# First loads in another order, and the last block of an encoder layer closed in two halves of 256 columns

## The chip, the cores and the metric

The kernel runs on one core of a Trainium2 chip. The metric is device time in microseconds (us) of one launch. Three runs of the kernel before took 1307.38, 1307.95 and 1308.11 us, so the median is 1307.95 us.

## What is computed

One encoder layer in float32 on 256 positions (two blocks of 128, called t = 0 and t = 1 here) with a width of 2048:

```python
def mixer_block(x, ...):
    h = rms_norm(x, g_norm)
    uv, qkv, gates = split(h @ w_in)
    y_a = gmlp_branch(uv, ...)            # gelu, LayerNorm, spatial gate
    y_b = neighbourhood_attn(q, k, v, rpb)
    g_a, g_b = split(sigmoid(gates))
    return x + (g_a * (y_a @ w_branch[:1024]) + g_b * (y_b @ w_branch[1024:])) @ w_out
def conv_ffn(x, ...):
    up = conv3(rms_norm(x, g) @ w_up)
    return x + (silu(gate) * val) @ w_down
out = rms_norm(conv_ffn(mixer_block(x)), norm_final)
```

The two ends matter here: the first product, which is the v columns of `h @ w_in`, and the last one, `@ w_down` with its residual, followed by the final RMSNorm.

## The kernel before, in words

**Three products for one.** Every float32 operand is split into a high and a low part in TensorE's fast float32 form. ScalarE (ACT) writes the high part, VectorE (DVE) subtracts it to get the low part, and TensorE (PE) does high x high, low x high and high x low (lines 289 to 291, helper `triple`). A weight piece is 128 rows by 1024 columns, 512 KB; SP loads it as `wraw` (line 126; the first piece in two DMAs of 512 columns, line 124), ACT writes `whi` (line 151) and DVE `wlo` (line 152). Pieces are numbered through the whole program. Five `wraw` buffers and four of `whi` and `wlo` each are turned over.

**The order of the work** is written out by hand. `begin(i)` is called ahead of the products of piece i: it issues the loads up to piece i + 5, does the splits up to piece i + 4 (for the first nine pieces up to the number in `SPLIT_TO`), and runs the tasks that `at(i, ...)` has put down for this piece. `preload[i]` names DMAs that go on SP's queue just ahead of the load of piece i. Each engine executes its instructions in the order in which they are written; SP's and ACT's DMA queues too.

**The start.** The first weight columns, v, are taken with the 16 slices of the transposed x in the order `V_ORDER` = 0, 1, 6, 7, 8, 9, 10, 11, 12, 13, 2, 3, ... Slice k is 128 x 256 values in `xr` (128 KB); `x_split(k)` multiplies it by the norm vector `gmix` and splits it (ACT line 495, DVE line 496, tile `h`). `x_chunk(c)` does slices 2c and 2c + 1; `X_TURN` lists the chunks c and the piece at which each is split, and the order of their loads. ACT's queue loads `gmix` (8 KB) and slice 1; SP's loads slice 0, piece 0 in two halves, piece 1, slices 6 and 7 together, piece 2, slices 2 and 3, piece 3, slices 8 and 9, piece 4, slices 10 and 11, piece 5 and so on. While the first data are on the way, `keep_awake` gives PE 17 transposes of the identity (`WAKE`, line 440).

For some pairs of pieces (`V_QUADS`, pieces 10 to 13 of v) a 2 x 2 block is done in seven products in place of eight. That needs sums of x slices (`act_sums`, lines 295 to 298 and 305, then split in lines 314 and 315) and of weights (lines 324 to 327 and 334, 335); `X_SUMS` says at which piece the sums of x are made. A first statistic of x (`x_norm`, lines 449 to 455) follows at piece 17 on DVE, and after it a gelu on ACT (line 548) with a table load.

**The end.** `run_wide` computes the last 1024 output columns of `@ w_down` in four accumulators `C[t][c]` of 128 x 512, one PSUM bank each. The last four weight pieces (`tail`) are kept back, and then done for one accumulator after the other, 12 products each, so that `finish` can take t = 0, c = 0; then t = 0, c = 1; then t = 1, c = 0; and last t = 1, c = 1. For each `finish` adds the residual (DVE, line 1023), takes the sum of squares (ACT, line 1026, accumulated), and multiplies by the final norm's weights into `y` (DVE, line 1063). After c = 1 follows the root: DVE `pt`, DVE `a` (lines 1069, 1070), ACT `q` = sqrt(a) (line 1071), DVE reciprocal and one Newton step (1072 to 1074). Then `write` scales the 2048 columns of this t in five cuts of 256, 512, 256, 512 and 512, on DVE (line 1085) or ACT (line 1083), and issues five DMAs to the output (line 1089). For t = 0 `write` is put off until after the add and the multiplication of t = 1, c = 0.

Of the kernel before, what the change touches and what calls it, by code (L numbers as in the profile page):

```python
# [8 lines left out]
F32 = mybir.dt.float32  # L9
F32R = mybir.dt.float32r  # L10
AF = mybir.ActivationFunctionType
# [52 lines left out]
def trunk_kernel(ctx, tc, x, x_t, vecs, w_in, ln_g, ln_b, w_st, b_s, rpb, w_branch, w_out, w_up, w_down,  # L64
# [105 lines left out]
    def at(i, f):  # L170
        tasks.setdefault(i, []).append(f)
# [168 lines left out]
    def run_wide(g, tail=0):  # L340
# [8 lines left out]
        def plain(i, t, c):  # L349
            h, l = split_t[i]  # L350
            triple(C[t][c], x_of(order[i - n0], t), h[:, c], l[:, c], i == n0, i == n1 - 1)

# [53 lines left out]

    xr = xin.tile([128, KD, T], F32, name="xr")

# [4 lines left out]
    def load_xt(k, n, queue=None):  # L413
        (queue or nc.sync).dma_start(xr[:, k:k + n], x_t[:, k:k + n])

    gmix = const.tile([128, KD], F32)
    gffn = const.tile([128, KD], F32)
    ck = const.tile([128, 4, 2 * NF], F32)
    nc.scalar.dma_start(gmix, vecs[:, 0:KD])
    load_xt(1, 1, nc.scalar)  # L420

    def load_late():
        nc.sync.dma_start(gffn, vecs[:, KD:2 * KD])
        nc.sync.dma_start(ck.rearrange("p a b -> p (a b)"), vecs[:, 2 * KD:])

# [629 lines left out]

    def finish(ps, t, c):
        x2 = rs["x2"]
        add_down(ps[t][c], t, 2 + c)
        square_columns(t, 2 + c)
        if c == 0:  # L1060
            fin["y", t] = hpool.tile([128, 2, 512], F32, name=f"h{t}")
        y = fin["y", t]
        nc.vector.tensor_mul(y[:, c], x2[:, t, 1024 + c * 512:1536 + c * 512], fin["g", 2 + c])
        if c == 0:
            if t:
                fin["out"]()
            return
        a, r, q, e, pt, both = (const.tile([128, 1], F32, name=f"{n}3{t}") for n in "arqepb")
        nc.vector.tensor_scalar(pt, fin["ss"][:, t, 2:3], 1.0 / D, fin["part"][:, t:t + 1], op0=OP.mult, op1=OP.add)
        nc.vector.tensor_scalar(a, fin["ss"][:, t, 3:4], 1.0 / D, pt, op0=OP.mult, op1=OP.add)  # L1070
        nc.scalar.activation(q, a, AF.Sqrt)
        nc.vector.reciprocal(r, q)
        nc.vector.scalar_tensor_tensor(e, r, r, a, op0=OP.mult, op1=OP.mult)
        nc.vector.tensor_scalar(e, e, -0.5, 1.5, op0=OP.mult, op1=OP.add)

        def write():
            on_act = (3,) if t else (1, 3)
            cuts = (0, 256, 768, 1024, 1536, 2048)
            for n in (0, 1, 2, 3, 4):
                v = x2[:, t, cuts[n]:cuts[n + 1]]  # L1080
                u = y[:, n - 3] if n > 2 else v
                if n in on_act:
                    nc.scalar.activation(v, u, AF.Copy, scale=both)
                else:
                    nc.vector.tensor_scalar(v, u, r, e, op0=OP.mult, op1=OP.mult)
                if n == 0:
                    nc.vector.tensor_mul(both, r, e)
            for n in (0, 1, 2, 3, 4):
                (nc.scalar if n == 3 else nc.sync).dma_start(out[0, t * 128:(t + 1) * 128, cuts[n]:cuts[n + 1]],
                                                             x2[:, t, cuts[n]:cuts[n + 1]])  # L1090

        if t:
            write()
        else:
            fin["out"] = write
# [64 lines left out]
    def down_order(g):  # L1160
# [5 lines left out]
    g_dn = [wide(w_d, 0, down_order(g), g * 1024, lambda k: ff["a"][k], DOWN_QUADS[g], down_room,  # L1166
                 (ev_sums(2 * g, down_room), ev_down if g == 0 else finish), stored=stored, split_room=both_rooms) for g in range(2)]
# [10 lines left out]
    for c, i in X_TURN[1:]:  # L1178
        at(i, lambda c=c: x_chunk(c))
# [111 lines left out]

    fin["ss"] = const.tile([128, NT, 4], F32, name="ss_3")
    at(g_dn[0][1] + 6, open_fin)
    def load_fin():
# [47 lines left out]
```

## Time and profile before

| what | value |
|---|---|
| median of three runs | 1307.95 us (1307.38 to 1308.11) |
| the profiled execution's own time | 1307.83 us |
| its span, first to last instruction | 1306.0 us |
| busy, PE / DVE / ACT / POOL | 1293.6 / 1072.5 / 776.8 / 104.7 us |
| mean granted TensorE clock | 0.997 |
| read from HBM, written | 266.48 MB, 7.34 MB |

A profile is one execution. The profiled execution lies within the three runs, and 1.8 us of its time are outside its span. Times in the trace count from the span's start. In its rows the first number is the start and the second the duration; `SPq` and `ACTq` are the instructions that issue DMAs, and a "landing" is the time from the start of that instruction until the data are in place. PE's matmuls overlap: a 128x512 product is listed with 389 ns, but the next begins 0.23 us after it.

### The profile page before, as it was taken

Reading aid. Unit: us, or ns where it says so; the run is one execution under the profiler, and the core shown is the slowest. Engines: PE = TensorE matmul, PEld = TensorE weight load, DVE = VectorE, ACT = ScalarE, POOL = GpSimd, SP = SyncE. Lnnn points to the kernel's source line nnn. Section 1 sums busy time; section 2 is a strip of 40 time slices with the busy share of each in tenths; the row PEclk is TensorE's granted clock in tenths of the full one; section 3 lists DMA queues with packets and bytes.
Section 4 is the critical chain, followed back from the end, with each engine's and each line's share of the span. In section 5 each row is a group of like instructions: output and inputs, shape, how many; then the busy total and the mean of one; then the engine's idle time right before and its main releaser. Section 6 shows DMA issues by size and latency. Waiting matters only on the chain.

```text
span 1306.0 us, 19254 instructions
## 1 busy us (share of the span) xinstructions
PE 1293.6 (99%) x6712; PEld 1103.9 (85%) x6712; DVE 1072.5 (82%) x1616; ACT 776.8 (59%) x1153; POOL 104.7 (8%) x206
## 2 busy tenths in 40 slices
PE   9999999999999999999999999999999999999997
PEld 7888888888888888888888888888888888888885
DVE  7997777667689966986778878787888889999997
ACT  7766476666655644556556556565555656665563
POOL 0005405413000000000000000000000000000000
PEclk9999999999999999999999999999999999999998
DMA  9779657556556657565566566666666658876782
GB/s 351 251 243 258 191 166 214 175 171 195 177 170 204 218 182 248 202 211 163 177 195 209 182 211 198 215 194 212 191 211 199 215 161 286 288 267 227 265 290 105
DMA packets 174225, 277.19 MB, mean 212 GB/s; under 512 B 13488, under 2 KB 121904, under 8 KB 174128
## 3 DMA queue, kind: packets, MB, share of 16 engines
q1 hardware_dynamic: 165520, 252.28, 59.5%
q0 software_dynamic: 8032, 23.03, 5.5%
q8 instruction: 52, 0.85, 0.3%
q10 hardware_dynamic: 576, 0.66, 0.1%
q14 instruction: 45, 0.37, 0.1%
HBM read 266.48 MB, written 7.34 MB: 210 GB/s over the span
## 4 chain that ended last, share of the span: by engine, by line
PE 96%; DVE 1%; ACT 1%; DMA 1%; issue 0%; SPq 0%; ACTq 0%; DVEq 0%
PE bank L203 31%; PE bank L207 16%; PE bank L291 11%; PE bank L289 11%; PE bank L290 11%; PE bank L231 5%; PE bank L233 4%; PE bank L232 4%; DMA wraw<-in_w_in_dram 1%; PE bank L756 1%; PE bank L806 0%; DVE wlo L152 0%; PE bank L622 0%; PE bank L796 0%; PE bank L887 0%
## 5 line engine op out<-in xcount | busy, mean ns | idle before, releaser
L152 DVE TENSOR_TENSOR wlo<-wraw,whi 128x1024 fp32r<-128x1024 f32 (+1 forms) x472 | 546.0, 1170 | 182.5 <-ACT whi L151 100.4
L151 ACT ACTIVATE whi<-wraw 128x1024 fp32r<-128x1024 f32 (+1 forms) x472 | 470.3, 1010 | 218.4 <-PE bank L290 85.1
L203 PE MATMUL bank<-h,whi 128*128 128x512 f32 x1760 | 425.5, 392 | 0.0
L203 PEld LDWEIGHTS bank<-h,whi 128*128 128x128 f32 x1760 | 322.1, 188 | 61.7
L207 PEld LDWEIGHTS bank<-h,wlo 128*128 128x128 f32 x1760 | 225.9, 191 | 8.8
L207 PE MATMUL bank<-h,wlo 128*128 128x256 f32 x1760 | 228.6, 283 | 0.0
L985 ACT ACTIVATE tc<-ta,ck 128x256 f32<-128x256 f32 x86 | 47.1, 594 | 117.1 <-DVE ta L983 117.1
L291 PE MATMUL bank<-wlo,a 128*128 128x512 f32 x224 | 87.3, 390 | 0.0
L290 PE MATMUL bank<-whi,a 128*128 128x512 f32 x224 | 87.2, 389 | 0.0
L289 PE MATMUL bank<-whi,a 128*128 128x512 f32 x224 | 87.1, 389 | 0.0
L289 PE MATMUL bank<-whi,h 128*128 128x512 f32 x210 | 82.4, 393 | 0.6 <-ACT h L495 0.6
L291 PE MATMUL bank<-wlo,h 128*128 128x512 f32 x210 | 81.9, 390 | 0.7 <-DVE wlo L152 0.7
L290 PE MATMUL bank<-whi,h 128*128 128x512 f32 x210 | 81.8, 390 | 0.8 <-DVE h L496 0.8
L334 ACT ACTIVATE h<-h 128x1024 fp32r<-128x1024 f32 x40 | 40.2, 1053 | 33.7 <-DVE h L326 33.7
L988 DVE SCALAR_TENSOR_TENSOR tc<-ta,ck,tc 128x255 f32<-128x255 f32 x86 | 41.4, 481 | 14.4 <-ACT tc L985 14.4
L231 PE MATMUL bank<-whi,y 128*128 128x512 f32 x128 | 50.5, 394 | 0.0
L231 PE MATMUL bank<-whi,h 128*128 128x512 f32 x128 | 50.4, 394 | 0.0
L233 PE MATMUL bank<-wlo,h 128*128 128x512 f32 x128 | 49.9, 390 | 0.0
L233 PE MATMUL bank<-wlo,y 128*128 128x512 f32 x128 | 49.9, 390 | 0.0
L232 PE MATMUL bank<-whi,y 128*128 128x512 f32 x128 | 49.8, 389 | 0.0
L232 PE MATMUL bank<-whi,h 128*128 128x512 f32 x128 | 49.8, 389 | 0.0
L291 PEld LDWEIGHTS bank<-wlo,a 128*128 128x128 f32 x224 | 42.0, 188 | 9.1 <-DVE wlo L152 0.3
(284 smaller groups left out, 1786.0 us busy)
## 6 DMA issues: line engine op xcount, KB each, us to landing
wraw<-in_w_up_dram SPq DMA_DIRECT2D x336, 256.0 KB, 3.2
wraw<-in_w_in_dram SPq DMA_DIRECT2D x111, 512.0 KB, 4.5
wraw<-in_w_down_dram SPq DMA_DIRECT2D x86, 512.0 KB, 5.4
wraw<-in_w_in_dram SPq DMA_DIRECT2D x66, 256.0 KB, 3.3
wraw<-in_w_branch_dram SPq DMA_DIRECT2D x32, 512.0 KB, 4.6
wraw<-in_w_out_dram SPq DMA_DIRECT2D x32, 512.0 KB, 4.0
h<-sums POOLq DMA_DIRECT2D x20, 512.0 KB, 7.0
sums<-so POOLq DMA_DIRECT2D x10, 512.0 KB, 5.4
```

The source lines that it names most:

```text
L151: nc.scalar.activation(h[:, k, :m], w[:, k, :m], AF.Copy)
L152: nc.vector.tensor_sub(l[:, k, :m], w[:, k, :m], h[:, k, :m].bitcast(F32))
L203: nc.tensor.matmul(p, h[:, k - k0, b * 128:(b + 1) * 128], acts(k), start=k == 0, stop=k == nk - 1)
L207: nc.tensor.matmul(p[:, :T], l[:, k - k0, b * 128:(b + 1) * 128], acts(k)[:, 0, :], start=False, stop=False)
L231: nc.tensor.matmul(p, xh, h[:, kk, :m], start=st, stop=False)
L232: nc.tensor.matmul(p, xl, h[:, kk, :m], start=False, stop=False)
L233: nc.tensor.matmul(p, xh, l[:, kk, :m], start=False, stop=sp)
L289: nc.tensor.matmul(p, xh, h, start=st, stop=False)
L290: nc.tensor.matmul(p, xl, h, start=False, stop=False)
L291: nc.tensor.matmul(p, xh, l, start=False, stop=sp)
L985: nc.scalar.activation(v, u, AF.Identity, scale=ck[:, 1, ch:ch + 1], bias=ck[:, 3, ch:ch + 1])
L988: nc.vector.scalar_tensor_tensor(v[:, 1:], u[:, :T - 1], ck[:, 0, ch:ch + 1], v[:, 1:], op0=OP.mult, op1=OP.add)
```

## The change

At the start: the norm vector is packed in front of the transposed x in memory, so that one DMA on ACT's queue brings it together with slice 0 (136 KB); SP starts with the weights. Slices 6 and 7 come in two DMAs of 128 KB, one ahead of piece 2 and one ahead of piece 3, and are split one by one, each ahead of the split of its piece. The chunks 8/9 and 10/11 go ahead of 2/3, and the sums of x for the seven-product blocks are made later. Three of the 17 transposes are left out.

At the end: the last block, t = 1, c = 1, is not continued in its bank. What its bank holds before the last four pieces is added to the residual first (`done[2]`, an `add_down` of 128 x 512). The products of the last four pieces go into fresh banks in two halves of 256 columns, each finished by itself. ACT takes the root straight from the sum of squares, with the division and the rest of the sum as scale and bias. In `write` ACT takes the third cut of t = 1, and the order of the output DMAs changes.

```diff
-WAKE = 17
+WAKE = 14
-X_TURN = ((0, 0), (3, 1), (1, 2), (4, 2), (5, 3), (2, 4), (6, 6), (7, 9))
-SPLIT_TO = (3, 4, 4, 7, 8, 8, 11, 12, 12)
+X_TURN = ((0, 0), (3, 1), (4, 2), (5, 3), (1, 4), (2, 5), (6, 6), (7, 9))
+SPLIT_TO = (2, 4, 4, 7, 8, 8, 11, 12, 12)
-X_SUMS = ((1, 3, 4), (2, 6, 9), (6, 18, 19))
+X_SUMS = ((1, 5, 6), (2, 7, 9), (6, 18, 19))
...
         for t in range(NT):
             for c in range(2):
+                if t and c:
+                    done[2](C[t][c])
+                    continue
                 for i in range(n1 - tail, n1):
...
-                done[1](C, t, c)
+                done[1](C[t][c], t, c, slice(0, 512))
+        for s in (slice(0, 256), slice(256, 512)):
+            p = bank()[:, :256]
+            for i in range(n1 - tail, n1):
+                h, l = split_t[i]
+                triple(p, x_of(order[i - n0], 1), h[:, 1, s], l[:, 1, s], i == n1 - tail, i == n1 - 1)
+            done[1](p, 1, 1, s)
...
-    nc.scalar.dma_start(gmix, vecs[:, 0:KD])
+    load_xt(0, 1, nc.scalar)
     load_xt(1, 1, nc.scalar)
...
-    def finish(ps, t, c):
+    def finish(p, t, c, s):
         x2 = rs["x2"]
-        add_down(ps[t][c], t, 2 + c)
-        square_columns(t, 2 + c)
+        v = x2[:, t, (2 + c) * 512 + s.start:(2 + c) * 512 + s.stop]
+        ss = fin["more"] if s.start else fin["ss"][:, t, 2 + c:3 + c]
+        nc.vector.tensor_add(v, p, v)
+        nc.scalar.activation(junk[:, :s.stop - s.start], v, AF.Square, accum_out=ss)
...
-        nc.vector.tensor_scalar(pt, fin["ss"][:, t, 2:3], 1.0 / D, fin["part"][:, t:t + 1], op0=OP.mult, op1=OP.add)
-        nc.vector.tensor_scalar(a, fin["ss"][:, t, 3:4], 1.0 / D, pt, op0=OP.mult, op1=OP.add)
-        nc.scalar.activation(q, a, AF.Sqrt)
+        if s.start == 0:
+            nc.vector.tensor_scalar(pt, fin["ss"][:, t, 2:3], 1.0 / D, fin["part"][:, t:t + 1],
+                                    op0=OP.mult, op1=OP.add)
+            fin["pt"] = pt
+        if s.stop < 512:
+            nc.vector.tensor_scalar(half, ss, 1.0 / D, pt, op0=OP.mult, op1=OP.add)
+            fin["pt"] = half
+            return
+        pt = fin["pt"]
+        nc.scalar.activation(q, ss, AF.Sqrt, scale=1.0 / D, bias=pt)
+        nc.vector.tensor_scalar(a, ss, 1.0 / D, pt, op0=OP.mult, op1=OP.add)
         nc.vector.reciprocal(r, q)
...
-            on_act = (3,) if t else (1, 3)
+            on_act = (2, 3) if t else (1, 3)
...
-    preload[0] = [lambda: load_xt(0, 1)]
-    for n, (c, _) in enumerate(X_TURN[1:]):
-        preload[n + 2] = [lambda c=c: load_xt(2 * c, 2)]
+    first_chunk = X_TURN[1][0]
+    preload[2] = [lambda: load_xt(2 * first_chunk, 1)]
+    preload[3] = [lambda: load_xt(2 * first_chunk + 1, 1)]
+    for n, (c, _) in enumerate(X_TURN[2:]):
+        preload.setdefault(n + 4, []).append(lambda c=c: load_xt(2 * c, 2))
...
+    at(1, lambda: x_split(2 * first_chunk))
+    at(1, lambda: split_to(3))
+    at(1, lambda: x_split(2 * first_chunk + 1))
-    laid["x_t"] = _np.asarray(inputs["x"])[0].T.reshape(KD, 128, T).transpose(1, 0, 2)
+    x_t = _np.asarray(inputs["x"])[0].T.reshape(KD, 128, T).transpose(1, 0, 2).reshape(128, KD * T)
+    laid["x_t"] = _np.concatenate([columns("norm_mix"), x_t], axis=1)
```

More of the change, by code (lines that the diff above doesn't have):

```diff
@@ L350, in plain @@
             h, l = split_t[i]
-            triple(C[t][c], x_of(order[i - n0], t), h[:, c], l[:, c], i == n0, i == n1 - 1)
+            last = n1 - 1 - (tail if t and c else 0)
+            triple(C[t][c], x_of(order[i - n0], t), h[:, c], l[:, c], i == n0, i == last)
         for i in range(n0, n1 - tail):
@@ L413, in load_xt @@
     def load_xt(k, n, queue=None):
[L414 to L416 removed]
+        c = slice(KD + k * T if k else 0, KD + (k + n) * T)
+        (queue or nc.sync).dma_start(xall[:, c], x_t[:, c])
     gffn = const.tile([128, KD], F32)
     ck = const.tile([128, 4, 2 * NF], F32)
[L419 removed]
+    load_xt(0, 1, nc.scalar)
     load_xt(1, 1, nc.scalar)
     def load_late():
[L423 to L424 removed]
+        nc.sync.dma_start(gffn, vecs[:, :KD])
+        nc.sync.dma_start(ck.rearrange("p a b -> p (a b)"), vecs[:, KD:])
     def load_ws():
@@ L1067, in finish @@
             return
-        a, r, q, e, pt, both = (const.tile([128, 1], F32, name=f"{n}3{t}") for n in "arqepb")
-        nc.vector.tensor_scalar(pt, fin["ss"][:, t, 2:3], 1.0 / D, fin["part"][:, t:t + 1], op0=OP.mult, op1=OP.add)
-        nc.vector.tensor_scalar(a, fin["ss"][:, t, 3:4], 1.0 / D, pt, op0=OP.mult, op1=OP.add)
-        nc.scalar.activation(q, a, AF.Sqrt)
+        small = [const.tile([128, 1], F32, name=f"{n}3{t}") for n in "phaqreb"]
+        pt, half, a, q, r, e, both = small
+        if s.start == 0:
[9 more added lines that the diff above has]
+        nc.vector.tensor_scalar(a, ss, 1.0 / D, pt, op0=OP.mult, op1=OP.add)
         nc.vector.reciprocal(r, q)
@@ L1087, in write @@
                     nc.vector.tensor_mul(both, r, e)
-            for n in (0, 1, 2, 3, 4):
-                (nc.scalar if n == 3 else nc.sync).dma_start(out[0, t * 128:(t + 1) * 128, cuts[n]:cuts[n + 1]],
+            for n in (0, 1, 4, 3, 2):
+                (nc.scalar if n in on_act and n != 1 else nc.sync).dma_start(out[0, t * 128:(t + 1) * 128, cuts[n]:cuts[n + 1]],
                                                              x2[:, t, cuts[n]:cuts[n + 1]])
@@ L1292, in trunk_kernel @@
     fin["ss"] = const.tile([128, NT, 4], F32, name="ss_3")
+    fin["more"] = const.tile([128, 1], F32, name="ss_4")
     at(g_dn[0][1] + 6, open_fin)
```

13 lines of the change are left out of this document (7 added, 6 removed).

## The prediction, made before the changed kernel ran

> **What bounds the kernel now.** I read the page first, then PE's waits over the whole span, then the chain of waits where the latest of them stands, and last the order of DVE's instructions ahead of it.
>
> ```profile
> span 1306.0 us, 19254 instructions
> PE 1293.6 (99%) x6712; PEld 1103.9 (85%) x6712; DVE 1072.5 (82%) x1616; ACT 776.8 (59%) x1153; POOL 104.7 (8%) x206
> ```
> ```profile
> PE bank L290 <- DVE h L496: 0.8, 1, 0.8
> PE bank L291 <- DVE wlo L152: 0.7, 2, 0.5
> PE bank L289 <- ACT h L495: 0.6, 1, 0.6
> ```
>
> PE is busy all the time except at both ends, and waits for data only four times (the transposes' wait for their identity left out). Three of these waits are in the first 20 us. The fourth, 0.5 us, comes later, and the chain of waits leads to it:
>
> ```profile
> 57.62 0.18 DVE n_a L449
> ...
> 62.34 1.28 ACT L548
> ...
> 64.87 0.96 ACT whi L151
> ...
> 65.86 1.24 DVE wlo L152
> ...
> 67.13 0.50 PE bank L291
> ```
>
> At 67.13 PE waits for a split that ACT could not begin before a table load and a gelu, and these waited for DVE. Now DVE's busy time in five stretches, of which the first and the last:
>
> ```profile
> 11.43:20.00 8.57, 8.50 (x16) 1.00 1.03 413
> 50.00:57.40 7.40, 7.37 (x11) 1.00 0.82 292
> ```
>
> With the three between them (9.90, 9.96 and 9.93 of 10 us) DVE works without a pause from 11.43 until the statistic at 57.62. **So what PE loses or gains in the first 20 us isn't what counts.** When PE gets going again at 67.13 is decided by how early DVE's unbroken work begins, how much it is, and whether holes come into it. After 67 us PE waits for nothing any more, and a shift there goes to the end unchanged. The second place is what follows PE's last product at 1296.63.
>
> **The change, part 1: the first loads.** Landings are an issue's start and the time to landing of the same issue.
>
> ```profile
> 1.37 3.89 PE L440 MATMUL bank<-ident 128*128 128x128 f32 x17 [1.37 <-POOL ident masks.py:199]
> 3.07 0.43 SPq L126 DMA_DIRECT2D wraw<-in_w_in_dram  x1
> 4.08 0.44 SPq L126 DMA_DIRECT2D wraw<-in_w_in_dram  x1
> 5.58 0.44 SPq L414 DMA_DIRECT2D xr<-in_x_t_dram  x1
> 6.75 1.15 ACT L151 ACTIVATE whi<-wraw 128x512 fp32r<-128x512 f32 x2 [0.66 <-DMA wraw<-in_w_in_dram]
> 10.34 1.06 ACT L151 ACTIVATE whi<-wraw 128x1024 fp32r<-128x1024 f32 x1 [2.44 <-DMA wraw<-in_w_in_dram]
> 11.43 1.22 DVE L152 TENSOR_TENSOR wlo<-wraw,whi 128x1024 fp32r<-128x1024 f32 x1 [2.73 <-ACT whi L151]
> 12.57 0.87 DVE L496 SCALAR_TENSOR_TENSOR h<-xr,gmix,h 128x256 fp32r<-128x256 f32 x2
> 16.39 2.94 ACT L151 ACTIVATE whi<-wraw 128x1024 fp32r<-128x1024 f32 x3
> ```
> ```profile
> wraw<-in_w_in_dram SPq DMA_DIRECT2D x1, 512.0 KB, 7.2
> wraw<-in_w_in_dram SPq DMA_DIRECT2D x1, 512.0 KB, 8.1
> xr<-in_x_t_dram SPq DMA_DIRECT2D x1, 256.0 KB, 9.2
> ```
>
> Piece 2 lands at 3.07 + 7.2 = 10.3, piece 3 at 4.08 + 8.1 = 12.2, slices 10/11 at 5.58 + 9.2 = 14.8. Between the first two lie 768 KB (slices 2/3, piece 3) in 1.9 us: 256 KB take 0.63 us. In the new order 128 KB fewer stand ahead of piece 2 (slice 7), and 256 KB fewer (slices 2/3) ahead of piece 3 and of slices 10/11. Estimated landings: 9.95, 11.6 and 14.15. SP's queue has one issue fewer (0.44 us) at its front, ACT's as many as before, POOL's none; the DMAs then run behind their issues by 7 to 9 us, so bytes and not issues decide. That the gmix DMA is gone gives nothing, slice 0 lands at the same time.
>
> Now DVE's stream, in the new order, for the same work up to the statistic. *Gains*: the low part of slice 6, 0.39 us (two in 0.87, each 0.48), moves into the hole of 2.73 us; the split of piece 2 begins with its landing, 0.35 us earlier. *New holes*: (a) at piece 4. ACT must now do slices 10 and 11 ahead of it, so DVE waits for 14.15 + 0.5 + 0.4 (two slices) + 1.05 (whi) = 16.1, while its own work since piece 2 (a split of 1024 columns 1.14, the distance of the rows at 11.43 and 12.57) would be done at 11.05 + 1.14 + 0.39 + 1.14 + 4 x 0.39 = 15.3: 0.8 us, of which 0.25 have gone already at piece 3 and slice 10. (b) at piece 8, behind the sums of x, which now stand right ahead of it: DVE makes them, ACT splits them (half a us, by their width), does two slices (0.8) and only then piece 8 (0.98 by 2.94 for three), 2.3 together, while DVE has the slices 4/5, the sums' low part and 12/13 to do, 4 x 0.39 and by its width 0.4 to 0.6, about 2.0: with the handover about 0.4 us of hole. Together 0.8 + 0.4 - 0.39 - 0.35 = **+0.45 us**: DVE's stream, and with it PE at 67, comes later, not earlier, although PE itself leaves the first 20 us about 1.2 us sooner. PE only waits longer at 67.
>
> The landing of slices 10/11 carries this. For each 0.1 us it is earlier or later, the stream is so too. Bounds: ACT begins on piece 1 at 6.75, when it has landed; from there to piece 2's landing at 10.3 the 768 KB of slices 6/7 and piece 2 took 3.55 us, the next 768 KB 1.9. If that slow stretch goes, landings are up to 1.65 us earlier than I estimate and the term is -1.2. If it comes twice, since slices 6 and 7 are now two DMAs with as many rows each, landings are up to 1.65 later and the term is +2.1. I take **+0.3**: nearest to the sum of the rows as they stand, less a little because the first bound has a reason (fewer bytes ahead of piece 2).
>
> A rule that speaks against the packing: by the Trainium skill's page "DMA: Bandwidth & Descriptors", section "How a descriptor splits into AXI transactions", reads go in 256 B steps from aligned addresses, and what lies before the start is fetched for nothing. With 64 B put in front of each row, by my estimate from that page three quarters of the rows fetch 64 to 192 B too much, about 70 KB until slices 10/11, 0.2 us later; the term would be +0.5 instead of +0.3. Every row is aligned before, so no row here shows it.
>
> Three transposes fewer end the warming at 1.37 + 14/17 x 3.89, about 4.6 instead of 5.26; the first product can then begin at about 4.8 (weights issued 0.44 earlier), and this too ends at the wait of piece 2. Cost at 67: nothing, as PE has over 2 us of room there.
>
> **Part 2: the end.** DVE and ACT behind the last products:
>
> ```profile
> 1294.33 0.69 DVE L1023 TENSOR_TENSOR x<-bank,x 128x512 f32<-128x512 f32 x1
> 1295.06 0.69 DVE L1063 TENSOR_TENSOR h<-x,gfin 128x512 f32<-128x512 f32 x1
> 1295.12 0.63 ACT L1026 ACTIVATE junk<-x 128x512 f32<-128x512 f32 x1 [1.40 <-DVE x L1023]
> ...
> 1296.39 0.54 DVE L1085 TENSOR_SCALAR x<-h,r,e 128x512 f32<-128x512 f32 x1
> 1296.63 0.39 PE L291 MATMUL bank<-wlo,a 128*128 128x512 f32 x1
> 1297.05 0.69 DVE L1023 TENSOR_TENSOR x<-bank,x 128x512 f32<-128x512 f32 x1
> 1297.94 0.63 ACT L1026 ACTIVATE junk<-x 128x512 f32<-128x512 f32 x1 [0.43 <-DVE x L1023]
> 1298.48 0.19 ACT L1026 ACTIVATION_READ_ACCUMULATOR junk<-x 128x1 f32 x1
> 1298.70 0.21 DVE L1070 TENSOR_SCALAR a<-ss,p 128x1 f32<-128x1 f32 x1
> 1298.95 0.20 ACT L1071 ACTIVATE q<-a 128x1 f32<-128x1 f32 x1 [0.28 <-DVE a L1070]
> 1299.18 0.17 DVE L1072 RECIPROCAL r<-q 128x1 f32<-128x1 f32 x1 [0.27 <-ACT q L1071]
> ```
> ```profile
> L977 DVE TENSOR_TENSOR ta<-bank,tb 128x256 f32<-128x256 f32 x86 | 30.5, 415 | 4.0 <-ACT tb L975 3.9
> L480 ACT ACTIVATE a<-tc 128x256 fp32r<-128x256 f32 x43 | 17.7, 411 | 18.9 <-DVE tc L996 18.9
> ```
>
> PE ends at 1296.63 + 0.39 = 1297.02, and DVE is only free at 1296.39 + 0.54 = 1296.93: both come together. The new products are 24 of 256 columns for 12 of 512; sixteen of that shape take 1.92 us from one group's start to the next, so 24 take 2.88 against 12 x 0.227 = 2.72:
>
> ```profile
> 801.57 2.08 PE L207 MATMUL bank<-h,wlo 128*128 128x256 f32 x16
> 803.49 3.82 PE L203 MATMUL bank<-h,whi 128*128 128x512 f32 x16
> ```
>
> PE ends 0.15 us later, but the first half is there at about 1295.7. **DVE can't take it**: it is in the outputs of t = 0 until 1296.93, and then the new add of what the old bank holds comes first. Step by step: that add at 1296.95; the add of the first half, which needs its result, 0.73 later (1294.33 to 1295.06) at 1297.68, for 0.415; ACT 0.10 behind its end (1295.02 to 1295.12), square and read 0.73 for 512 columns (1297.94 to 1298.67) less 0.22 for 256 (0.63 to 0.41), so until 1298.72; on DVE the new small step `half` stands at its place in the queue for this sum, at 1298.75, and the second half's add, long ready on PE, only behind it at 1298.92, until 1299.34; ACT square and read 1299.44 to 1299.95; root on ACT right behind, 0.20 to 0.30 with the pointer as bias; reciprocal at 1300.2 instead of 1299.18. The step that goes (`a` and two handovers, 1298.67 to 1298.95, 0.28 us) and the shorter squares are less than one 0.73 add and a second add, square and read in series. **+1.05 us.** Behind the reciprocal DVE has a cut of 256 less and ACT one more; the outputs' 1 MB is written by DMAs that are full until the last, so I count about nothing, -0.05: +1.0. Bounds: +0.7, if DVE's gaps are shorter than I take them; +1.4, if the extra ACT cut holds back both its DMAs by an issue (0.35).
>
> **Sum**: 0.3 + 1.0 = +1.3 us on the profiled execution's 1307.83, so 1309.1; against the median of 1307.95, 0.09% more. A measurement of this kernel can't tell about 0.2%, 2.6 us, from no change.
>
> **The rivals.**
> *A, the loads come faster* (the slow stretch goes): start -1.2, end +1.0: 1307.6. For it: bytes ahead of piece 2 fall, and no row says why 768 KB took 3.55 us. Against: as many first rows must be read. 0.22.
> *B, the end does what it says*: if DVE reached the halves before PE's end, the root would follow PE by one add, square and root: 1297.17 + 0.52 + 0.52 + 0.25 = 1298.45, 0.7 less than 1299.18; with the start in the middle of +0.3 and -1.2, 1306.7. Against it stands 1296.93, which the change leaves where it is. 0.12.
> *C, slower beyond 0.2%*: slices 6 and 7 each pay the slow stretch, slices 10/11 land at 15.8 instead of 14.15, and DVE's hole at piece 4 grows by as much: +2.1 and +1.0: 1310.9. It decides from a landing of 15.3 on, where start and end together pass 2.6. 0.12.
> *D, the clock*: the first product took 0.78 us, the later ones of its shape 0.39:
>
> ```profile
> 5.23 0.78 PE L289 MATMUL bank<-whi,h 128*128 128x512 f32 x1
> ```
>
> If PE ran at half speed for 10 us more, its 1.2 us and the room at 67 would be spent, and each further product of 512 columns would cost 0.2 us: 1310 to 1312. Against it: three transposes fewer are 0.7 us less of 3.89, and the products that follow keep PE busy themselves. 0.03. The Trainium skill's page "TensorE: Matmul & The Clock Gate", section "What's actually happening", has PE at half rate until it was busy for a window of about 3.4 us; 14 transposes fill 3.2. By that rule one lost window is hidden by the wait at 67, so the sum stays, and only this chance stands for it.
>
> **How the numbers follow.** The forecast has 0.51, with 1308.3 to 1310.0 as its own range. A to D have 0.49. From 1306.4 to 1310.6 the forecast, most of A, half of B and a third of C are inside, about 0.8. Faster than 1305.2: 0.04 (A and B together at their ends: 1307.83 - 1.2 - 0.7 = 1305.9, and a little beyond); slower than 1310.6: 0.09 (most of C, D); within: 0.87.
>
> **What would show it.** Right: piece 2's first products earlier by about a microsecond, PE's wait near 67 grown to over 2 us; DVE with holes ahead of pieces 4 and 8, and its statistic at 57.6 to 58.4; the 512-column add at about 1296.95 plus that shift, and the last reciprocal 2.9 to 3.2 us behind the products' old end rather than 2.2. Wrong: slices 10/11 landed before 13.4; a statistic of DVE before 57; the halves' adds waiting for PE rather than for DVE.

## The result, and the profile after

The changed kernel took 1312.6 us in the median of five runs (1311.6 to 1313.75), against 1307.95 before (1307.27 to 1308.11): a ratio of 1.0038, with a 95% interval of 1.0023 to 1.0052. It is slower, by more than the forecast's 1309.1 and beyond its range. The profiled execution took 1311.6 us and is the fastest of the five; it is 3.77 us longer than the one before (1307.83), and those 3.77 us can be laid out completely.

First the page of the changed kernel, and PE's waits over its whole span (engine and line, what it waited for, total, times, longest):

```profile
span 1309.8 us, 19280 instructions
PE 1295.5 (99%) x6721; PEld 1103.7 (84%) x6721; DVE 1073.8 (82%) x1619; ACT 777.9 (59%) x1156; POOL 105.7 (8%) x206
```
```profile
PE bank L291 <- DVE wlo L152: 1.9, 2, 1.4
PE bank L451 <- POOL ident masks.py:199: 1.4, 1, 1.4
PE bank L289 <- ACT whi L151: 1.1, 2, 0.8
```

PE's waits for data are 3.0 us in all, 0.9 more than in the rows of before, and none is later than 67.37 us. But PE is *busy* 1.9 us longer, with three transposes fewer and 12 products of 512 columns turned into 24 of 256. So the larger part of the loss is in no wait. It is found by laying PE's instructions of the two traces side by side, counted back from the end of t = 1, c = 0, and looking where the distance grows: 0.24 us at 67.4; 0.5 at 336; then steadily to 1.5 at 380; flat until 466; steadily to 2.7 at 508; flat to the end. The two slopes are exactly the products with y as stationary operand. The groups by form (busy, mean ns of one; a product's end is modelled, so the mean moves with the distance to the next), before, then after:

```profile
L231 PE MATMUL bank<-whi,y 128*128 128x512 f32 x128 | 50.5, 394 | 0.0
L233 PE MATMUL bank<-wlo,y 128*128 128x512 f32 x128 | 49.9, 390 | 0.0
L232 PE MATMUL bank<-whi,y 128*128 128x512 f32 x128 | 49.8, 389 | 0.0
```
```profile
L231 PE MATMUL bank<-whi,y 128*128 128x512 f32 x128 | 51.1, 400 | 0.0
L232 PE MATMUL bank<-whi,y 128*128 128x512 f32 x128 | 50.6, 395 | 0.0
L233 PE MATMUL bank<-wlo,y 128*128 128x512 f32 x128 | 50.5, 395 | 0.0
```

Each takes 5 to 6 ns more. In the order of time (start, duration) the changed kernel's products begin 0.233 to 0.234 us apart, where before they began 0.227 apart. Before:

```profile
470.13 0.39 PE L232 MATMUL bank<-whi,y 128*128 128x512 f32 x1
...
470.81 0.39 PE L232 MATMUL bank<-whi,y 128*128 128x512 f32 x1
...
471.50 0.39 PE L232 MATMUL bank<-whi,y 128*128 128x512 f32 x1
```

After:

```profile
469.74 0.40 PE L232 MATMUL bank<-whi,y 128*128 128x512 f32 x1
...
470.44 0.39 PE L232 MATMUL bank<-whi,y 128*128 128x512 f32 x1
...
471.14 0.40 PE L232 MATMUL bank<-whi,y 128*128 128x512 f32 x1
```

Three products in 0.68 or 0.69 us before, 0.70 after. Over the 414 products behind 67 us that have y as an operand the distances of starts add up to +2.4 us; all of PE between 67 us and the last block gives +2.49. No instruction of these lines was touched by the diff. What the diff did to them is their address: const lost the 64 bytes of `gmix` and got 96 (`half` for both t, `more`), each small tile taking 32. So every tile allocated on the low side (whi, wlo, h and what follows) lies 32 bytes higher, while y, on the high side, stays.

Then the two places of the forecast. The start, from the chain of waits; DVE's order near 20 to 30 us is in the point by point part:

```profile
57.86 0.18 DVE n_a L460
...
66.09 1.24 DVE wlo L152
...
67.37 0.50 PE bank L291
```

67.37 against 67.13: +0.24 us. One pair of profiles is a small sample for this term. In the eight profiles on record with the old start (before and seven kernels of the experiments below) this product begins between 66.61 and 67.52 us, in the seven with the new start between 67.25 and 67.79; the means are 67.07 and 67.47, so +0.40. The end, DVE's and ACT's rows:

```profile
1297.06 0.69 DVE L1071 TENSOR_TENSOR x<-bank,x 128x512 f32<-128x512 f32 x1 [0.15 <-PE bank L291]
1299.57 0.69 DVE L1034 TENSOR_TENSOR x<-bank,x 128x512 f32<-128x512 f32 x1
1300.36 0.42 DVE L1071 TENSOR_TENSOR x<-bank,x 128x256 f32<-128x256 f32 x1
1301.47 0.21 DVE L1088 TENSOR_SCALAR h<-ss,p 128x1 f32<-128x1 f32 x1
1301.60 0.42 DVE L1071 TENSOR_TENSOR x<-bank,x 128x256 f32<-128x256 f32 x1
1302.65 0.30 ACT L1092 ACTIVATE q<-ss,h 128x1 f32<-128x1 f32 x1
1302.98 0.16 DVE L1094 RECIPROCAL r<-q 128x1 f32<-128x1 f32 x1
```

From the add of t = 1, c = 0 to the last reciprocal it is 5.92 us; before, 1294.33 to 1299.18, 4.85. That is +1.07. From the reciprocal to the end of the span both kernels take 6.8 us. **0.24 + 2.49 + 1.07 = 3.80**, against the 3.77 between the two executions.

### The profile page after: what moved, and what is told of

Same layout as the page of the kernel before. It is cut to its first block, busy times and chain, and to the rows that moved or that the text cites. A ratio compares the mean times of both kernels' runs of the same rounds, so it can differ in the third digit from the quotient of the medians.

```text
span 1309.8 us, 19280 instructions
## 1 busy us (share of the span) xinstructions
PE 1295.5 (99%) x6721; PEld 1103.7 (84%) x6721; DVE 1073.8 (82%) x1619; ACT 777.9 (59%) x1156; POOL 105.7 (8%) x206
## 4 chain that ended last, share of the span: by engine, by line
PE 95%; DVE 2%; DMA 2%; ACT 1%; issue 0%; SPq 0%; DVEq 0%; ACTq 0%
PE bank L203 31%; PE bank L207 16%; PE bank L291 11%; PE bank L289 11%; PE bank L290 11%; PE bank L231 5%; PE bank L233 5%; PE bank L232 4%; DMA wraw<-in_w_in_dram 2%; DVE wlo L152 1%; PE bank L767 1%; PE bank L817 0%; PE bank L633 0%; PE bank L807 0%; PE bank L970 0%
## 5 line engine op out<-in xcount | busy, mean ns | idle before, releaser
L291 PE MATMUL bank<-wlo,a 128*128 128x512 f32 (+1 forms) x228 | 88.0, 386 | 0.0
L290 PE MATMUL bank<-whi,a 128*128 128x512 f32 (+1 forms) x228 | 87.9, 385 | 0.0
L289 PE MATMUL bank<-whi,a 128*128 128x512 f32 (+1 forms) x228 | 87.8, 385 | 0.0
L291 PE MATMUL bank<-wlo,h 128*128 128x512 f32 x210 | 82.1, 391 | 1.9 <-DVE wlo L152 1.9
L289 PE MATMUL bank<-whi,h 128*128 128x512 f32 x210 | 82.1, 391 | 1.1 <-ACT whi L151 1.1
L290 PE MATMUL bank<-whi,h 128*128 128x512 f32 x210 | 81.7, 389 | 0.0
L232 PE MATMUL bank<-whi,y 128*128 128x512 f32 x128 | 50.6, 395 | 0.0
L231 PE MATMUL bank<-whi,h 128*128 128x512 f32 x128 | 50.4, 394 | 0.0
L289 PEld LDWEIGHTS bank<-whi,a 128*128 128x128 f32 x228 | 42.8, 188 | 8.6
L290 PEld LDWEIGHTS bank<-whi,a 128*128 128x128 f32 x228 | 42.8, 188 | 8.5
```

The costliest lines, as they stand in the source:

```text
L231: nc.tensor.matmul(p, xh, h[:, kk, :m], start=st, stop=False)
L232: nc.tensor.matmul(p, xl, h[:, kk, :m], start=False, stop=False)
L289: nc.tensor.matmul(p, xh, h, start=st, stop=False)
L290: nc.tensor.matmul(p, xl, h, start=False, stop=False)
L291: nc.tensor.matmul(p, xh, l, start=False, stop=sp)
```

## The experiments

Two theories stood at first. *Layout*: the pace of a product depends on where its two operands lie, and the 32 bytes in const cost 2.5 us. *Order*: the new start shifts when DVE, ACT and DMAs work beside PE, and this slows PE. "Before" is the median of the kernel before, measured beside it on the same chip.

### Moving y, or the rest

```diff
 # after_y192: the changed kernel;  before_y192, before_y160: the kernel before
-Y_GAP = 224
+Y_GAP = 192      # before_y160: 160
 # after_const96: the changed kernel, Y_GAP 224
     fin["more"] = const.tile([128, 1], F32, name="ss_4")
+    const.tile([128, 24], F32, name="pad")
```

> The changed kernel, only Y_GAP 192 for 224: the tiles y move up by 32 bytes, and lie against the low side's tiles (whi, wlo, h, const) again as they did before the change, which put 32 bytes more into const. Layout theory: the 384 products with y as the stationary operand (lines 231 to 233) go back from 234 to 227 ns apart, and the 30 of lines 289 to 291 with them, 2.5 us less: profiled run 1309.1, median 1309 to 1310.2. Rival (the new order of the start shifts when DVE, ACT and DMAs work beside PE, and this slows the products): nothing changes, 234 ns, 1311.6 to 1313.

> The changed kernel, with 96 more bytes in const (a tile that nobody uses), so that everything on the low side lies 128 bytes higher than before the change and y where it was. Layout theory: 227 ns for the products with y, 1309 to 1310.2, as with Y_GAP 192, since only the distance of the two sides counts, and it is a multiple of 128 again. Rival (order of the start): 234 ns, 1311.6 to 1313. A third, that the low side's addresses must be as before to the byte: 1311.6 to 1313 too, but Y_GAP 192 then as well.

> The kernel before, only Y_GAP 192 for 224: y lies 32 bytes higher, nothing else moves, no instruction changes. Layout theory: lines 231 to 233 with y at 234 ns instead of 227, 2.5 us more: 1310.2 to 1311. Rival (order of the start): 1307.9, unchanged.

> The kernel before, Y_GAP 160 for 224: y lies 64 bytes higher. Layout theory doesn't say the step that counts: if it is 64 bytes, 227 ns and 1307.9; if it is 128 bytes, 234 ns or between and 1310 to 1311. Rival (order of the start): 1307.9.

| run | y above before's place / low side above it | line 232, mean ns | median, us | before | ratio (95%) |
|---|---|---|---|---|---|
| after_y192 | +32 / +32 | 389 | 1310.73 | 1308.43 | 1.0020 (1.0011 to 1.0029) |
| after_const96 | 0 / +128 | 395 | 1312.93 | 1308.43 | 1.0034 (1.0021 to 1.0047) |
| before_y192 | +32 / 0 | 395 | 1310.72 | 1308.43 | 1.0018 (1.0009 to 1.0027) |
| before_y160 | +64 / 0 | 395 | 1311.24 | 1308.43 | 1.0023 (1.0014 to 1.0032) |

The kernel before, with one constant changed and not one instruction, loses 2.3 us and gets the same slow rows; here is its L232:

```profile
L232 PE MATMUL bank<-whi,y 128*128 128x512 f32 x128 | 50.6, 395 | 0.0
```

And the changed kernel with y moved after the rest has the fast ones back:

```profile
L232 PE MATMUL bank<-whi,y 128*128 128x512 f32 x128 | 49.8, 389 | 0.0
```

*Order* has fallen. *Layout* stands, but its form was wrong: 128 bytes between the sides (after_const96) and 64 are as bad as 32. after_y192's profile has one more wait, which PE's rows of 100 to 200 us show and which comes and goes in other kernels too, some of before's own variants among them:

```profile
PE bank L203 <- DVE ya L637: 0.5, 1, 0.5
```

### The pace by itself

Stretches of 60 products in the pattern of lines 231 to 233, on two tiles, one shifted against the other; in some DVE and ACT work beside them. Nothing of the layer is computed, and each of the two kernels was executed once. Of the loop, shortened:

```python
for n, (dm, ds, dd, dma) in enumerate(SECTIONS):      # shifts in bytes
    m, s = dm // 4, ds // 4
    for j in range(20):
        hi, lo = sta[:, s:s + 128], sta[:, s + 128:s + 256]
        h, l = mov[:, m:m + 512], mov[:, m + 512:m + 1024]
        nc.tensor.matmul(p, hi, h, ...); nc.tensor.matmul(p, lo, h, ...); nc.tensor.matmul(p, hi, l, ...)
```

> No part of the layer is computed here, the output is zeros: only 20 stretches of 60 products of 512 columns in the pattern of lines 231 to 233, all on the same two tiles, with the moving operand shifted by 0, 4, 16, 32, 64, 128, 256, 512 bytes, the stationary one by 0, 32 or 64, and in the later stretches DVE and ACT working beside PE on other tiles at shift 0 or 32. Theory a, the distance of PE's own two operands counts: 227 ns apart at 0/0, 32/32 and 64/64, about 234 at 32/0 and 0/32, whoever works beside. Theory b, the distance of PE's operands to what DVE and ACT read and write counts: 227 in all quiet stretches, 234 where PE is at 0 and DVE and ACT at 32 or the reverse. If all stretches show 227, neither, and something else that goes with the addresses (DMA writes, the high region) has to be looked for.

> As the run with products alone (nothing of the layer is computed, zeros out), all stretches quiet, with more shifts of one operand against the other and with products of 256 and 128 columns. If the step is 256 bytes: 227 ns at 256, 512, 1024, 2048 and at 128/128, 238 at 8, 233 at 32 and again at 288 and 1056 (32 beyond a multiple), 229 at 64 and again at 0/64, 232 at 128 and at 384; shift of the stationary operand by 32 like shift of the moving one by 224. If the true step is 512 or more, 256 was luck: then 1056 or 384 differ from 32 and 128. Products of 256 columns: 120 ns at 0; the loss is either the same 6 ns for each product, or half of it as it goes with the columns.

The mean distance of starts, without the first twelve of a stretch, from both runs:

```
moving ahead of stationary by (bytes)    ns     |  by     ns   |  both shifted / beside   ns
0, 256, 512, 1024, 2048                  226.7  |  96    233.4 |  32/32, 64/64, 128/128   226.7
4                                        237.9  |  112   231.3 |  0/0, DVE+ACT at 0, 32   226.7
8                                        232.2  |  128   232.5 |  32/0, DVE+ACT at 0, 32  233.3
16                                       231.6  |  160   234.4 |  96/32                   228.9
32, 288, 1056                            233.3  |  192   233.4 |  0/32 (= 224)            233.3
64                                       228.8  |  224   233.4 |  240                     236.7
256 columns: 0, 256: 120.0;  32: 116.6;  64: 117.8;  128: 118.7.   128 columns: 111.6 at 0 and at 128, 111.7 at 32
```

(128 gave 232.5 in one run and 233.4 in the other. In the full kernel y is the stationary operand: y 64 bytes higher, as in before_y160, is 192 in this table and not 64.) Theory a holds: what counts is the distance of PE's own two operands, modulo 256 bytes; what DVE and ACT touch doesn't matter. Rows of the first run with 32 between the operands, DVE and ACT at work (first), and with 0 (second):

```profile
200.11 0.40 PE L104 MATMUL bank<-mov,sta 128*128 128x512 f32 x1
...
200.81 0.39 PE L104 MATMUL bank<-mov,sta 128*128 128x512 f32 x1
```
```profile
20.04 0.39 PE L105 MATMUL bank<-mov,sta 128*128 128x512 f32 x1
...
20.72 0.39 PE L105 MATMUL bank<-mov,sta 128*128 128x512 f32 x1
```

Behind the break at the head of a stretch, the first three to ten distances of starts are uneven at distance 0 as well, and most of them longer than 227 ns. That would explain why products on y and y, such as the nine at 75 us, are slow too, though both operands lie on the side that stays and the same products began 227 ns apart before: they stand between badly placed ones. No run has them by themselves. The last expectation of pace_table, the sign at 256 columns, was wrong both ways: of the four distances measured there, 0 is the *slowest*.

The step of 256 in the full kernel:

```diff
-Y_GAP = 224
+Y_GAP = 480
```

> The kernel before, only Y_GAP 480 for 224: y lies 256 bytes lower, no instruction changes. If the distance of the two operands counts modulo 256: 227 ns for the products with y, ratio 1.000 (1307.5 to 1308.8). If y has to lie where it was: 234 ns and 2.3 to 2.5 us more, as with 192 and 160.

1308.12 beside 1308.04, ratio 0.9998 (0.9989 to 1.0007), line 232 at 389 ns: y may lie elsewhere, if it is by 256.

### Start and end apart, with the layout of before

Each kernel has the small tiles of the end put together, or unused bytes in const, so that the large tiles lie as before. root_only's edit:

```diff
-        nc.vector.tensor_scalar(a, fin["ss"][:, t, 3:4], 1.0 / D, pt, op0=OP.mult, op1=OP.add)
-        nc.scalar.activation(q, a, AF.Sqrt)
+        nc.scalar.activation(q, fin["ss"][:, t, 3:4], AF.Sqrt, scale=1.0 / D, bias=pt)
+        nc.vector.tensor_scalar(a, fin["ss"][:, t, 3:4], 1.0 / D, pt, op0=OP.mult, op1=OP.add)
```

> The whole change, with two small tiles of the end put together and 64 unused bytes in const, so that the large tiles of both sides lie at the addresses that they have before the change (a few tiles behind xr apart). Layout theory: products with y 227 ns apart again; left are start and end as forecast, +0.3 and +1.0: 1309 to 1309.8 beside a kernel before of 1308 (ratio 1.0005 to 1.0015). Rival (only Y_GAP's own place counts): 234 ns and 1312.

> Only the start of the change, end and layout as before. My steps: +0.3 (bounds -1.2 and +2.1): ratio 1.0002; DVE's statistic 0.2 to 0.5 us later, PE's wait near 67 grown. Rival A of the forecast (loads faster): -1.2, ratio 0.999. Rival (the start alone also shifts later waits on DVE, such as the one near 140 us in other profiles): +1 and more in the median, with PE waits after 70 us in the profile.

> Only the end of the change, start and layout as before. My steps: +1.0, ratio 1.0008, last reciprocal 5.9 us behind the add of t = 1, c = 0 (4.85 before). Rival B (DVE reaches the halves as PE makes them): -0.7, ratio 0.9995.

> The kernel before, only the root taken by ACT straight from the sum of squares (scale and bias), DVE's step a behind it; no halves, no other order. My steps: ACT's root begins at the end of its read instead of 0.28 us later, its scale and bias cost up to 0.1: -0.2 to -0.28, ratio 0.9998, last reciprocal 4.6 us behind the add of t = 1, c = 0 instead of 4.85. Rival (the DMAs of the output, not the root, set the end): no change, with the reciprocal earlier and the last DMA as late as before.

| run | median, us | before | ratio (95%) | in the profile |
|---|---|---|---|---|
| all_same_layout | 1309.83 | 1308.03 | 1.0012 (1.0003 to 1.0021) | y products 389 ns; reciprocal 5.92 behind the add |
| start_only | 1308.42 | 1308.03 | 1.0004 (0.9995 to 1.0013) | the last split ahead of PE's wait ends at 67.39, 67.09 before |
| end_only | 1309.32 | 1308.03 | 1.0012 (1.0003 to 1.0020) | reciprocal 5.91 behind the add |
| root_only | 1308.43 | 1308.03 | 1.0004 (0.9995 to 1.0013) | 4.69 instead of 4.85; ACT's root 0.30 long, not 0.20 |

The whole change without the layout costs 1.8 us in the medians (0.4 to 2.7 by its interval), where start and end forecast 1.3; the changed kernel as it is, 4.65. end_only's median holds time that no row shows: up to 3.4 us of its runs lie outside the span, in no other kernel more than 2.3. By the spans its median is 0.6 us above before's (1306.9 and 1306.3). The root alone brings the reciprocal 0.16 us forward, and in the time nothing that can be told.

### What the end's 1.07 us are

```diff
 # add_early: all_same_layout, done[2] ahead of the last four pieces
+        done[2](C[1][1])
         for t in range(NT):
...
                 if t and c:
-                    done[2](C[t][c])
                     continue
 # halves_free: add_early, and half made only behind the second half's add and multiplication
         if s.stop < 512:
-            nc.vector.tensor_scalar(half, ss, 1.0 / D, pt, op0=OP.mult, op1=OP.add)
             return
+        if s.start:
+            nc.vector.tensor_scalar(half, fin["ss"][:, t, 3:4], 1.0 / D, pt, op0=OP.mult, op1=OP.add)
```

> As the whole change with the layout of before, but the new 512-column add of t = 1, c = 1 stands on DVE ahead of the adds of the last four pieces' results, where it has nothing to hold up, not between t = 0's outputs and the first half. My steps: the first half's add 0.73 us earlier, the second half by what PE's end allows, last reciprocal 5.2 us behind the add of t = 1, c = 0 instead of 5.92: 0.7 us less than the whole change with this layout (1309.83 beside 1308.03), so ratio 1.0006 to 1.0010. Rival (the halves themselves cost it, two adds, squares and reads in series): no gain, 1.0012 to 1.0015.

> As the run with the early add, but the two small DVE steps p and half stand behind the second half's add and multiplication instead of ahead of them, so that no step that waits for ACT's square of the first half stands ahead of the second half's add. If this order holds up the rest (my reading of the early-add run: 0.65 us of DVE waiting there), the last reciprocal comes about 4.9 to 5.2 us behind the add of t = 1, c = 0 instead of 5.66, and the ratio is 1.0004 to 1.0009. Rival (ACT, which has t = 0's outputs and both squares, is late by itself): 5.5 to 5.7 and 1.0010 to 1.0013.

add_early: 1309.75 beside 1308.18, ratio 1.0011 (1.0002 to 1.0020). Not 0.73 but 0.26 us came back (reciprocal 5.66 behind the add of t = 1, c = 0). DVE's rows show where the rest stayed:

```profile
1297.77 0.42 DVE L1071 TENSOR_TENSOR x<-bank,x 128x256 f32<-128x256 f32 x1
...
1299.42 0.21 DVE L1090 TENSOR_SCALAR p<-ss,p 128x1 f32<-128x1 f32 x1 [0.65 <-ACT junk L1072]
1299.55 0.42 DVE L1071 TENSOR_TENSOR x<-bank,x 128x256 f32<-128x256 f32 x1
```

The 128x1 step `half` (tile p here) waits for ACT's square of the first half, and the second half's add, whose products are done, stands behind it. ACT itself is late: it begins that square at 1298.88, 0.69 us after the first half's add has ended, right behind the issue of a DMA of t = 0's outputs (0.35 us from 1298.48 on). In halves_free only `half` (1299.11 here) goes behind the second half's add and multiplication; the expectation speaks of two steps, but p stays where it was (1298.19). 1308.68 beside 1308.16, ratio 1.0003 (0.9994 to 1.0012):

```profile
1294.89 0.69 DVE L1071 TENSOR_TENSOR x<-bank,x 128x512 f32<-128x512 f32 x1
...
1297.40 0.42 DVE L1071 TENSOR_TENSOR x<-bank,x 128x256 f32<-128x256 f32 x1
...
1298.19 0.21 DVE L1086 TENSOR_SCALAR p<-ss,part 128x1 f32<-128x1 f32 x1
1298.32 0.41 DVE L1071 TENSOR_TENSOR x<-bank,x 128x256 f32<-128x256 f32 x1
...
1299.11 0.21 DVE L1093 TENSOR_SCALAR p<-ss,p 128x1 f32<-128x1 f32 x1
...
1299.91 0.16 DVE L1098 RECIPROCAL r<-q 128x1 f32<-128x1 f32 x1
```

5.02 us from the add of t = 1, c = 0 to the reciprocal, as expected. Taken off in this order, the add's place in DVE's queue was worth 0.26 of the 1.07, and the place of `half`, one step of one column, 0.64. The 0.17 left are not a gain either. The rival's numbers are out, though ACT is late in both runs: its first square begins 3.61 us behind the add of t = 1, c = 0 here as there. What changed is that DVE no longer stands still for it.

### Using the pace

Of 256 columns there are 1760 products in the kernel (line 207), in turns of 16 long (line 203) and 16 short ones. pace_turns makes such turns alone, with the short ones' stationary tile shifted (zeros out, nothing of the layer):

> Nothing of the layer, zeros out: turns of 16 products of 512 columns and 16 of 256, as lines 203 and 207 take them in the up projection; the operands of the 512-column ones 0 apart (modulo 256), the stationary operand of the 256-column ones shifted by 0, 32, ... 224 in the successive stretches, 0 again at the end. In the table of shifts, 256 columns took 120.0 ns at 0 and 116.6 at 32. If that holds between the long ones, a turn of 16 and 16 is 0.05 us shorter with a shift (110 such turns in the kernel, 5 us). Rival: the first long products behind misplaced short ones give it back, and a turn is as long as at 0, 5.55 us, or longer.

A turn took 5.567 us at 0, and at 32, 64, 96, 128, 160, 192, 224: 5.573, 5.540, 5.533, 5.567, 5.580, 5.573, 5.527. At 32 the rival holds: the long products behind give all of it back. At 96 and 224 a net gain stays. So a version of the kernel before with that:

```diff
+LOW_AT = (0, 128, 0, 128, 96, 96, 96, 96)      # low_long: (0, 128, 0, 128) twice
-            l = wpool.tile([128, 2, 512], F32R, name="wlo", bufs=SPLIT_AHEAD + 1)
+            o = LOW_AT[i % 4 + 4 * (i in stat)] // 4      # stat: pieces whose low part is stationary
+            l = wpool.tile([128, 1056], F32R, name="wlo", bufs=SPLIT_AHEAD + 1)
+            l = l[:, o:o + 1024].rearrange("p (a b) -> p a b", b=512)
```

> The kernel before, computing all of it, with wlo tiles 128 bytes longer, and the low parts that serve as stationary operand of the 256-column products (line 207 before) written 96 or 224 bytes (modulo 256, turn about) away from their moving operand; every 512-column pair stays 0 apart, y where it was. By the run with turns, where a turn took 5.533 at 96 and 5.527 at 224 instead of 5.567 us, 110 turns give 3.6 to 4.4 us less: 1303.6 to 1304.6 beside 1308.1, ratio 0.9966 to 0.9973, short products about 117 ns apart. Rival (other waits, of DVE or the loads, take over as soon as PE is faster): part of it or nothing, with PE waits after 70 us in the profile.

> The control to it: the same longer wlo tiles, but every low part 0 apart from its partner modulo 256. If the placing modulo 256 is all that counts: ratio 1.000 (1307.6 to 1308.6), 120 ns. If the longer tiles themselves change something, it shows here.

**low_shifted took 1306.38 us** beside 1308.36, ratio 0.9984 (0.9975 to 0.9993), and beats both kernels; low_long, the same tiles with every pair at 0, 1307.88, ratio 0.9996 (0.9988 to 1.0005). Rows of low_shifted (its line 207 has the long ones, 211 the short), to be set against the rows of the kernel before at 801.57 and 803.49:

```profile
801.70 2.03 PE L211 MATMUL bank<-h,wlo 128*128 128x256 f32 x16
803.57 3.84 PE L207 MATMUL bank<-h,whi 128*128 128x512 f32 x16
807.24 2.03 PE L211 MATMUL bank<-h,wlo 128*128 128x256 f32 x16
```

Sixteen short ones take 1.87 us for 1.92, the long ones 3.67 instead of 3.65: 0.03 less for this turn. Over all 110 turns of the two profiles the starts of the short ones lie 4.4 us closer together, and those of the long ones behind them 2.2 us further apart, so the pace gains 2.2 us. The medians show 2.0 against before and 1.5 against low_long, the control; 3.6 to 4.4 were expected. In the profile one wait near 140 us, not counted in the 2.2, takes 0.9, though what brings it on in this execution is not settled:

```profile
PE bank L207 <- DVE ya L630: 0.9, 1, 0.9
```

## Why the prediction was wrong

**The step that failed** is this one of the first part: "After 67 us PE waits for nothing any more, and a shift there goes to the end unchanged." The first half is true of the changed kernel's profile (no wait after 67.37), the second isn't: the sum held PE's pace for untouched products to be given. The prediction went through the edits by what they issue, wait for and read, and passed over what they *allocate*: `half`, `more` and the vanished `gmix` move the low side by 32 bytes. Missing term: +2.49 us in the profile; 2.3 in before_y192, where nothing else changed.

**The start**, +0.3, measured +0.24 in this pair of profiles, +0.40 in the means of all, and +0.4 in the medians of start_only, which is not clear of noise. That the sum fits is luck in part, since two of its terms were off and cancelled out. Slices 10/11 landed at 5.84 + 7.6 = 13.4, not 14.15 (piece 2 at 9.1, not 9.95), so rival A's faster loads came true in part. By "for each 0.1 us ... the stream is so too" the term should have been -0.3. But behind the split of piece 2 DVE met four holes, not two:

```profile
15.38 2.36 DVE L152 TENSOR_TENSOR wlo<-wraw,whi 128x1024 fp32r<-128x1024 f32 x2 [0.46 <-ACT whi L151]
17.91 1.23 DVE L152 TENSOR_TENSOR wlo<-wraw,whi 128x1024 fp32r<-128x1024 f32 x1 [0.17 <-ACT whi L151]
24.61 2.96 DVE L152 TENSOR_TENSOR wlo<-wraw,whi 128x1024 fp32r<-128x1024 f32 x3 [0.27 <-ACT whi L151]
28.48 0.69 DVE L325 TENSOR_TENSOR y<-y,wraw 128x512 f32<-128x512 f32 x1 [0.31 <-DMA wraw<-in_w_in_dram]
```

The ones at pieces 4 and 8 (0.46, 0.27) are those forecast as 0.8 and 0.4. They stand in all seven profiles with the new start, within 0.01 us; the others come and go. Laid out for this profile: DVE's work begins 1.21 us earlier (10.22 for 11.43) and has one slice less to do (0.40), but loses 1.35 to idle time and about 0.5 to instructions that follow each other less closely (four slices at 13.10 take 1.81 us where they took 1.67), which is +0.24. The last hole waits for a load, and the chain of waits says why it can't be earlier:

```profile
19.16 9.23 DMA wraw<-in_w_in_dram
```

That load is issued at 19.16, when the split that began at 17.91 has ended and a buffer comes free, and takes 9.2 us behind the others; from 10 to 30 us the DMA engines are full, both rows of this view of the stretches show a share of 1.03:

```profile
10.00:20.00 10.00, 10.00 (x46) 8.29 (x45) 8.97 (x13) 8.33 (x14) 0.00 (x0) 1.00 1.03 401
20.00:30.00 10.00, 10.00 (x46) 8.29 (x45) 9.35 (x17) 8.18 (x16) 0.00 (x0) 1.00 1.03 401
```

DVE worked 18.3 of these 20 us. As these rows read, its stream can start earlier, but not run ahead of a full queue: the gain is bounded by bytes, not by the first landing alone. No run tested this by itself. PE's lead (2.1 us at 19.5, forecast 1.2) went for the most part in a wait of 1.4 us that ended at 40.56, not at 67 as forecast, where the wait stayed 0.5.

**The end**, +1.0, measured +1.07, in the sequence that the prediction wrote down, `half` ahead of the second add included. It gave the price to the 512-column add and the doubled steps; the runs give 0.26 to the add's place and 0.64 to that of `half`.

**Rivals.** B is out: the first half's add waited for DVE, 0.8 us behind the row at 1299.57, not for PE. C's sign came true by another mechanism. D's mechanism came true in some executions, its price didn't. In the changed kernel's profile the first products were not slow; the first took 0.50 us, before's 0.78:

```profile
5.41 0.50 PE L289 MATMUL bank<-whi,h 128*128 128x512 f32 x1 [0.79 <-ACT whi L151]
5.75 0.40 PE L290 MATMUL bank<-whi,h 128*128 128x512 f32 x1
```

But four of the seven profiles with 14 transposes (after_y192, after_const96, add_early, halves_free) begin their first seven to ten products 0.43 us apart and only then 0.23, as here in after_y192:

```profile
6.50 0.63 PE L291 MATMUL bank<-wlo,h 128*128 128x512 f32 x1
6.93 0.63 PE L289 MATMUL bank<-whi,h 128*128 128x512 f32 x1
7.36 0.63 PE L290 MATMUL bank<-whi,h 128*128 128x512 f32 x1
```

In these four the record of a fully granted clock begins at 8.9 to 10.1 us of the span, in the other three at 4.8 to 5.0, and with 17 transposes, where at most three products are so slow, at 4.1 to 6.9. By the rule weighed there (the Trainium skill, "TensorE: Matmul & The Clock Gate", "What's actually happening") PE runs at half rate until it was busy for a window of about 3.4 us. The traces agree in part: 3.25 us of transposes were too little in four profiles of seven but enough in three, and in low_long the full clock came 2.7 us after the first transpose. The wait at 67 hides most of it, as the forecast said: there the four are 0.2 us later on average than the three, and the profiles of one start differ by 0.5 and more.

**What stays open.** The median lies 1.0 us above the profiled run. The waits on ya near 140 us that other profiles have (0.4 to 0.9) would fit, but the one profile of the changed kernel shows none. Three of the four profiles with the late clock have that wait, none of the three others with 14 transposes, but also three of the eight with 17; what brings it on stays open. The packing's cost was not run by itself; it is +0.2 by the estimate from the Trainium skill's page "DMA: Bandwidth & Descriptors", section "How a descriptor splits into AXI transactions".

## What to carry to other kernels

When a change adds or removes even a 32-byte tile, look which tiles move against which, and compare the distance of starts of untouched products before looking for waits: a slower pace is in no list of waits. Keep the moving and the stationary operand of 512-column products in the fast float32 form a multiple of 256 bytes apart, and try 96 or 224 for products of 256 columns between them; with 128 columns no distance tried made a difference. Look at more than one profile before you call a rival out: here the clock at the start came early in some executions and late in others of the same instructions. And a one-column step that waits for another engine is as long as that wait for all that stands behind it in its queue.

## What the runs showed of the hardware that was not expected

The distance of PE's two operands modulo 256 bytes sets the pace of back-to-back 512-column products in the fast float32 form: 226.7 ns at 0, 229 to 238 elsewhere; for 256 columns the order is turned round at the four distances measured, 120.0 at 0 and 116.6 at 32. The Trainium skill's page "TensorE: Matmul & The Clock Gate", section "Step-by-step: what each phase is for", says that PE has two independent read ports, so that loading the next weights doesn't take read bandwidth from the running product. The runs differ: without any other engine at work, the same products on the same tiles take 226.7 or 233.3 ns by nothing but that distance, so the pace does depend on where the two operands lie. By which mechanism, no run tells.
